# A decoder layer on one core: attention and w_out's first half put in an order written by hand

## Chip, core and metric

One core of one Trainium2 chip runs the whole layer in one launch. The metric is the device time of one execution in microseconds, the median over several runs.

## What is computed

One decoder layer on x of 512 positions by 1024 channels, in float32, cut to what matters here:

```python
h = rms_norm(x, g_pre_mix)
q, k, v, xr, gr = split(h @ w_in, ...)              # five parts of 512 columns
logits = q @ k.T * 64**-0.5 + bias[t5_bucket(q_pos - k_pos)]   # 8 heads of 64, causal
attn = softmax(logits) @ v
lru  = rg_lru(causal_dwconv(xr)) * gelu(gr)         # recurrent group
x = x + rms_norm(concat([attn, lru]) @ w_out, g_post_mix)
h = rms_norm(x, g_pre_ffn)
x = x + rms_norm((gelu(c_g) * c_u) @ w_down, g_post_ffn)       # c_u, c_g = conv3(h @ w_up)
```

With 512 positions and blocks of 256, of which up to three past ones are picked, the block-sparse attention of the reference is ordinary causal attention.

## The kernel before

**Products.** Every float32 operand of a product is held as two parts, an upper one (a rounded copy, made by ScalarE) and a lower one (the difference, made by VectorE): `split`, and for weights `split_w`. A product is then three matmuls, upper by upper, upper by lower and lower by upper (`mm3`, lines 79 to 81). Weights come by DMA into one of two `raw` buffers and are split into one of four `wh` and four `wl` slots.

**Stages.** Input norm and transposition into hT; the recurrent group's projection, convolution and gates; v; gr; then attention (up to line 702), the output product w_out in two halves of 512 columns (`wide`, for n = 0 and 1) with the post-norm, and the feed-forward part (w_up, w_down). Everything up to line 578 stands in an order written by hand for TensorE, ScalarE, VectorE and SP (`manual_schedule`, closed by `written.close()`). From there on a planner that estimates costs decides the order in which each engine gets its instructions.

**Attention.** Heads go in four pairs. `head_pair(pr)` loads the bias rows `tb` and the pair's q and k weights, splits the weights, makes 2 x 8 projection products (24 matmuls for q, 24 for k), and casts: q into its upper half (ScalarE) and lower half (VectorE), k into two copies of the upper half (ScalarE) and the lower half `klz` (VectorE), for each head s = 0, 1. A tile is 128 query positions of one head: 32 tiles (pr, s, i), and tile i sees 128 (i + 1) keys. `softmax` (lines 629 to 648) makes two score matmuls, adds the bias and takes the row maximum (one VectorE instruction, L640), negates and scales the maximum (L643), exponentiates with row sums (ScalarE, L644), takes the reciprocal (L646) and multiplies (L647, here the quotient). `transposed` turns the tile by TensorE (i + 1 transposes into `ptp`) and splits it into `pTh` and `pTl`. After the four tiles of a head `attend` makes eight value matmuls into `pav`, copies one half (ScalarE) and adds the other (VectorE) into `pair`, and splits `pair` into mixT.

The loop over the 32 tiles makes scores LAG = 3 tiles ahead of their transposes, and after each of them takes FILL = 3 projection products of the next pair. The products of w_out's first half (`py`, 4 row blocks x 8 k x 3 matmuls, banks "mm", "mm", "mm", "av") follow in program order; the planner may move them forward.

**PSUM.** Eight banks: three "mm" (projections, w_out), two "sc" (scores), two "tr" (transposes), one "av" (values).

**After attention.** `wide` for n = 1 splits the second half's weights, runs t by t, and `mixed` makes each row block's post-norm, the norm before the feed-forward part and its transposes into h2T. In between `load_first_up` loads and splits the first weights of w_up (`fw00` to `fw11`).

Of the kernel before, what the change touches and what calls it, by code (L numbers as in the profile page):

```python
# [39 lines left out]
ISCALE = DH ** -0.5  # L40
FE = S + P
EW = 3 * P
FILL = 3
LAG = 3
assert MAX_DISTANCE <= P

# [6 lines left out]
def hybrid_layer(  # L53
# [515 lines left out]
    for t in range(NT):  # L569
        pg = bank("pgr", "mm")  # L570
        for k in range(KD):
            mm3(pg, at(w_gr[t], slice(None), k), at(hT, slice(None), k), k == 0, k == KD - 1)
        if t >= 2:
            first_w.append(split_w(first_qk[:, :, t - 2], KD, P))
# [17 lines left out]
    heads = {}  # L592
# [5 lines left out]
    def head_pair(pr):  # L598

        tb = ap_.tile([P, 2, S], F32, tag="tb", name="tb")  # L600
# [6 lines left out]
        if pr:  # L607
            raw = load_qk(pr)
        ws = [split_w(raw[:, :, i], KD, P) for i in range(2)] if pr else first_w
        yield  # L610

        proj = []
        for w in ws:
            pq = bank("pq", "mm")
            for k in range(KD):
                mm3(pq, at(w, slice(None), k), at(hT, slice(None), k), k == 0, k == KD - 1)
                yield
            proj.append(pq)
        qs, ks = (ap_.tile([P, 2, S], F32R, tag=f"s{i}", name=f"s{i}") for i in "qk")
        kl = klz  # L620
        for s in range(2):
            me, other = own[s], own[1 - s]
            nc.scalar.copy(qs[me, s], proj[0][me])
            nc.vector.tensor_sub(qs[other, s], proj[0][me], f32(qs[me, s]))
            nc.scalar.copy(ks[me, s], proj[1][me])
            nc.scalar.copy(ks[other, s], proj[1][me])
            nc.vector.tensor_sub(kl[me, s], proj[1][me], f32(ks[me, s]))
        heads[pr] = qs, ks, kl, tb

    def softmax(pr, s, i):  # L630

        qs, ks, kl, tb = heads[pr]
# [3 lines left out]
        nc.tensor.matmul(psc[:, :W], qs[:, s, qi], ks[:, s, :W], start=True, stop=False)
        nc.tensor.matmul(psc[:, :W], qs[:, s, qi], kl[:, s, :W], start=False, stop=True)
        st = ap_.tile([P, S], F32, tag="st", name="st", bufs=4)
        sm = ap_.tile([P, 12], F32, tag="sm", name="sm", bufs=4)
# [7 lines left out]
        nc.vector.tensor_scalar(st[:, :W], st[:, :W], sm[:, 3:4], None, op0=ALU.mult)  # L647
        return st

    def transposed(st, pT, i):  # L650
        ptr = bank("ptp", "tr")
        for j in range(i + 1):
            nc.tensor.transpose(ptr[:, j * P:(j + 1) * P], st[:, j * P:(j + 1) * P], ident)  # L653
        split(by_keys(pT[0], i), by_keys(pT[1], i),
              ptr[:, :P * (i + 1)].rearrange("p (j q) -> p j q", q=P))

    def attend(pr, s, pT, pair):
        me, other = own[s], own[1 - s]
        pav = bank("pav", "av")
        for j in range(NT):  # L660
            vs = vhl[:, j, pr, 2 * s:2 * s + 2].rearrange("p a d -> p (a d)")
            for i in range(2):
                nc.tensor.matmul(  # L663
                    pav[:, j * P:], vs, pT[i][:, j * S:j * (S - P) + S],
                    start=j == 0 and i == 0, stop=j == NT - 1 and i == 1)
        nc.scalar.copy(pair[me], pav[other])
        nc.vector.tensor_add(pair[me], pav[me], pair[me])
        if s == 1:
            split(mixT[0][:, pr], mixT[1][:, pr], pair)

    tiles = [(pr, s, i) for pr in range(NPAIR) for s in range(2) for i in range(NT)]
    for _ in head_pair(0):
        pass
    ahead, sts, last = iter(()), [], None
    for n in range(-LAG, len(tiles)):
        if 0 <= n + LAG < len(tiles):
            pr, s, i = tiles[n + LAG]
            if s == 0 and i == 0:  # L680
                for _ in ahead:
                    pass
                if pr + 1 < NPAIR:
                    ahead = head_pair(pr + 1)
                    next(ahead)
            sts.append(softmax(pr, s, i))
        for _ in itertools.islice(ahead, FILL):
            pass
        if n < 0:
            continue  # L690
        pr, s, i = tiles[n]
        if i == 0:
            if last:
                attend(*last)
            if s == 0:
                pair = ap_.tile([P, S], F32, tag="pair", name="pair", bufs=1)
            pT = [ap_.tile([P, 3 * (S - P) + S], F32R, tag=f"pT{j}", name=f"pT{j}", bufs=1)
                  for j in "hl"]
            last = pr, s, pT, pair
        transposed(sts.pop(0), pT, i)  # L700
# [198 lines left out]
```

## Time and profile before

| | |
|---|---|
| median of 3 runs | 585.64 us (584.77 to 586.01) |
| profiled execution | 584.45 us |
| its span, first to last instruction | 582.3 us |
| TensorE matmul busy | 571.0 us (98%), 2734 matmuls |
| VectorE / ScalarE / GpSimd busy | 360.1 / 279.3 / 15.9 us |
| granted TensorE clock, mean | 0.996 |

The profile shows one execution. Matmul rows are longer than the distance of their starts, since matmuls are pipelined, so a busy share near 100% can hold waits; distances of starts show them. Releasers are inferred from semaphore events.

### The profile page before, as it was taken

What the parts mean: (1) busy time and instruction counts of PE and PEld (TensorE: products, weight loads), DVE (VectorE), ACT (ScalarE), POOL (GpSimd) and SP (SyncE); (2) the same over time, 40 slices, a digit from 0 to 9 for tenths busy, and PEclk for the clock granted to TensorE, in tenths of its full rate; (3) what the DMA queues carried; (4) which work ended last, traced back from release to release, by engine and by line L of the source; (5) the groups of instructions that cost most, each with busy time, mean ns of one, the idle gap of its engine ahead of it and who ended that gap; (6) DMA issues with size and microseconds to landing.
All of it is one profiled execution on the core that took longest, in us unless ns stands there. A gap on an engine that the chain in (4) does not pass through costs nothing.

```text
span 582.3 us, 7051 instructions
## 1 busy us (share of the span) xinstructions
PE 571.0 (98%) x2734; PEld 472.9 (81%) x2734; DVE 360.1 (62%) x649; ACT 279.3 (48%) x457; POOL 15.9 (3%) x37
## 2 busy tenths in 40 slices
PE   8999999999999999999999999999999999999995
PEld 4988887887788789888888888888888888888884
DVE  5797777889896895656656656656656521241225
ACT  6568846868776663543443444444444321132121
POOL 2150000000000000000000000000000000000000
PEclk9999999999999999999999999999999999999998
DMA  9533627333202614013412412412413222332103
GB/s 275 152 110 122 205 72 200 94 106 108 74 1 72 217 41 142 1 49 96 145 55 90 144 60 86 146 64 81 144 66 136 88 72 90 100 136 73 37 0 144
DMA packets 53450, 59.62 MB, mean 102 GB/s; under 512 B 2481, under 2 KB 42625, under 8 KB 53418
## 3 DMA queue, kind: packets, MB, share of 16 engines
q1 hardware_dynamic: 53319, 59.11, 31.9%
q8 instruction: 21, 0.34, 0.2%
q14 instruction: 12, 0.09, 0.1%
q10 hardware_dynamic: 98, 0.07, 0.0%
HBM read 57.06 MB, written 3.69 MB: 104 GB/s over the span
## 4 chain that ended last, share of the span: by engine, by line
PE 90%; DVE 4%; ACT 3%; DMA 2%; issue 0%; DVEq 0%; SPq 0%; ACTq 0%
PE pup L80 14%; PE pup L81 14%; PE pup L79 14%; PE py L80 8%; PE py L79 8%; PE py L81 8%; PE px L309 3%; PE pq L79 2%; PE pq L80 2%; PE pq L81 2%; PE pav L663 2%; PE ptp L653 1%; PE pgr L81 1%; PE pgr L80 1%; PE pv L81 1%; PE pv L80 1%
## 5 line engine op out<-in xcount | busy, mean ns | idle before, releaser
L85 DVE TENSOR_TENSOR wl<-raw,wh 128x1024 fp32r<-128x1024 f32 x78 | 95.3, 1222 | 125.4 <-ACT wh L84 125.1
L84 ACT CAST wh<-raw 128x1024 fp32r<-128x1024 f32 x78 | 81.7, 1049 | 139.7 <-PE py L81 71.7
L80 PE MATMUL pup<-h2Tl,wh 128*128 128x512 f32 x320 | 124.5, 389 | 0.0
L81 PE MATMUL pup<-h2Th,wl 128*128 128x512 f32 x320 | 124.5, 389 | 0.0
L79 PE MATMUL pup<-h2Th,wh 128*128 128x512 f32 x320 | 124.3, 389 | 0.0
L80 PEld LDWEIGHTS pup<-h2Tl,wh 128*128 128x128 f32 x320 | 60.1, 188 | 12.5
L79 PEld LDWEIGHTS pup<-h2Th,wh 128*128 128x128 f32 x320 | 60.0, 188 | 12.5
L81 PEld LDWEIGHTS pup<-h2Th,wl 128*128 128x128 f32 x320 | 60.1, 188 | 12.3
L79 PE MATMUL py<-wh,acth 128*128 128x512 f32 x176 | 68.5, 389 | 0.0
L80 PE MATMUL py<-wl,acth 128*128 128x512 f32 x176 | 68.5, 389 | 0.0
L81 PE MATMUL py<-wh,actl 128*128 128x512 f32 x176 | 68.5, 389 | 0.0
L79 PEld LDWEIGHTS py<-wh,acth 128*128 128x128 f32 x176 | 33.0, 188 | 6.9
L81 PEld LDWEIGHTS py<-wh,actl 128*128 128x128 f32 x176 | 33.0, 188 | 6.9
L80 PEld LDWEIGHTS py<-wl,acth 128*128 128x128 f32 x176 | 33.0, 188 | 6.7
L821 DVE SCALAR_TENSOR_TENSOR yu<-pup,par,yu 128x511 f32<-128x511 f32 (+1 forms) x44 | 32.9, 749 | 4.3 <-ACT yu L819 3.5
L828 ACT ACTIVATE yg<-yg 128x512 f32<-128x512 f32 x22 | 13.9, 632 | 44.6 <-DVE yg L821 44.6
L821 DVE SCALAR_TENSOR_TENSOR yg<-pup,par,yg 128x511 f32<-128x511 f32 (+1 forms) x44 | 32.8, 746 | 2.0 <-ACT yg L819 1.2
L829 DVE TENSOR_TENSOR yu<-yu,yg 128x512 f32<-128x512 f32 x22 | 15.2, 693 | 18.0 <-ACT yg L828 18.0
L81 PE MATMUL py<-wh,mixTl 128*128 128x512 f32 x64 | 25.4, 397 | 0.0
L79 PE MATMUL pq<-hTh,wh 128*128 128x512 f32 x64 | 25.4, 397 | 0.0
L81 PE MATMUL pq<-hTh,wl 128*128 128x512 f32 x64 | 25.3, 395 | 0.0
L79 PE MATMUL py<-wh,mixTh 128*128 128x512 f32 x64 | 25.2, 394 | 0.0
(213 smaller groups left out, 938.2 us busy)
## 6 DMA issues: line engine op xcount, KB each, us to landing
raw<-in_w_up_dram SPq DMA_DIRECT2D x22, 1024.0 KB, 5.1
raw<-in_w_down_dram SPq DMA_DIRECT2D x10, 1024.0 KB, 5.3
raw<-in_w_in_dram SPq DMA_DIRECT2D x4, 1024.0 KB, 5.2
rawqk<-in_w_in_dram SPq DMA_DIRECT2D x8, 512.0 KB, 5.3
raw<-in_w_out_dram SPq DMA_DIRECT2D x4, 1024.0 KB, 5.6
raw<-in_w_in_dram SPq DMA_DIRECT2D x4, 512.0 KB, 9.1
out_dram<-yz SPq DMA_DIRECT2D x8, 256.0 KB, 2.0
xres<-in_x_dram SPq DMA_DIRECT2D x3, 512.0 KB, 5.8
```

Source lines behind the costliest of these rows:

```text
L79: nc.tensor.matmul(o, lh, rh, start=start, stop=False)
L80: nc.tensor.matmul(o, lh, rl, start=False, stop=False)
L81: nc.tensor.matmul(o, ll, rh, start=False, stop=stop)
L84: nc.scalar.copy(h, src)
L85: (sub or nc.vector).tensor_sub(l, src, f32(h))
L309: nc.tensor.matmul(p_x[t][:, cs], w_x[t][i == LH][:, k], hT[i == HL][:, k, cs], start=first and n == 0, stop=last and n == len(todo) - 1)
L653: nc.tensor.transpose(ptr[:, j * P:(j + 1) * P], st[:, j * P:(j + 1) * P], ident)
L663: nc.tensor.matmul(pav[:, j * P:], vs, pT[i][:, j * S:j * (S - P) + S], start=j == 0 and i == 0, stop=j == NT - 1 and i == 1)
L821: nc.vector.scalar_tensor_tensor(y[:, d:], pt[:, :S - d], w_conv_f(2 - d, blk), y[:, d:], op0=ALU.mult, op1=ALU.add)
L828: nc.scalar.activation(yg, yg, AF.Gelu_apprx_tanh)
L829: nc.vector.tensor_mul(yu, yu, yg)
```

## The change

GpSimd is given here as `nc.gpsimd`, VectorE as `nc.vector`. The written order, which ended after gr, now goes on through attention and through all of w_out's first half, and ends there. FILL is gone. `head_pair`, `softmax`, `transposed` and `attend` are cut into their steps; the loop names at every step n (-3 to 31) which steps are issued, for all engines in one text. One step stands for one tile n (transposes and halves) and for tile m = n + 3 (scores, maximum, exponential) and m - 1 (quotient).

- The negation L643 is gone: the maximum instruction now scales by -1/8 and takes the minimum, and the exponential scales by -1.
- Weights of pairs 2 and 3 and the four weight units of w_out's first half have their lower parts made by GpSimd (`w_split(..., nc.gpsimd)`, `out_split`): eight instructions. Those of pairs 0 and 1 stay with VectorE.
- q and k of the next pair are cast at chosen steps (o = n mod 8): q at o = 0 and 4, k at o = 3 and 6; their scores come at o = 5 and, for the second head, o = 1.
- The halves of a head's first tile come one step later (`late`), behind the value products of the head before.
- w_out's first half: loads at steps 5 and 13, splits at 15, 16, 19 and 24, products at steps 19 to 31 and after the loop; the fourth row block is in an "sc" bank.
- Pair 1's q and k weights are loaded right after pair 0's, two biases at the start.
- The second half's `wide` gets the banks "sc", "av", "mm", "mm"; the four drains of the first half (`weighted`) stand outside `wide`.

```diff
-    first_qk = load_qk(0)
+    raw_qk = {0: load_qk(0), 1: load_qk(1)}
...
-    written.close()
...
+    def w_split(pr, i, eng=None):
+        w_qk[pr, i] = split_w(raw_qk[pr][:, :, i], KD, P, eng)
...
+    def maxima(m):
+        pr, s, i = tiles[m]
+        W = P * (i + 1)
...
         nc.vector.tensor_tensor_reduce(
-            out=st[:, :W], in0=psc[:, :W], in1=tb[:, s, S - W:S], scale=1.0, scalar=NEG,
-            op0=ALU.add, op1=ALU.max, accum_out=sm[:, 0:1])
-        nc.vector.tensor_scalar(sm[:, 1:2], sm[:, 0:1], -ISCALE, None, op0=ALU.mult)
-        nc.scalar.activation(st[:, :W], st[:, :W], AF.Exp, scale=ISCALE, bias=sm[:, 1:2],
-                             accum_out=sm[:, 2:3])
+            out=sts[m][:, :W], in0=psc[m][:, :W], in1=tbs[pr][:, s, S - W:S], scale=-ISCALE,
+            scalar=-NEG, op0=ALU.add, op1=ALU.min, accum_out=sms[m][:, 0:1])
+
+    def exponentials(m):
+
+        st, sm = sts[m][:, :P * (tiles[m][2] + 1)], sms[m]
+        nc.scalar.activation(st, st, AF.Exp, scale=-1.0, bias=sm[:, 0:1], accum_out=sm[:, 2:3])
...
+    def out_split(u):
+        w_out0[u] = split_w(raw_out[u // 4][:, u % 4:u % 4 + 2], 2, 512, nc.gpsimd)
+
+    def out_piece(t, k):
+        if t not in p_out:
+            p_out[t] = bank(f"py{t}", "sc" if t == 3 else "mm")
+        mm3(p_out[t], at(mixT, slice(None), k, slice(t * P, (t + 1) * P)),
+            at(w_out0[k // 2 * 2], slice(None), k % 2), k == 4, k == 3)
...
+    PIECES = (1, 3, 2, 2, 1, 3, 2, 2)
+    OUT = {19: ((0, 4), (0, 5)), 20: ((0, 6),), 21: ((0, 7), (1, 4), (1, 5)),
+           22: ((1, 6), (1, 7)), 23: ((2, 4), (2, 5)), 24: ((2, 6),), 25: ((2, 7), (0, 0)),
+           26: ((0, 1), (1, 0)), 27: ((1, 1), (2, 0)), 28: ((2, 1),), 29: ((0, 2), (1, 2)),
+           30: ((2, 2), (3, 4)), 31: ((3, 5), (3, 6))}
+    bias(0)
+    bias(1)
+    raw_qk[2] = load_qk(2)
+    pieces(0, KD)
+    w_split(1, 0)
+    cast_q(0, 0)
+    cast_q(0, 1)
+    w_split(1, 1)
+    raw_qk[3] = load_qk(3)
+    pieces(0, KD)
+    cast_k(0, 0)
+    pieces(1, 3)
+    late = None
     for n in range(-LAG, len(tiles)):
...
+        pr, o, m = n // 8, n % 8, n + LAG
+        if n >= 0:
+            turned(n)
+        if m < len(tiles):
+            scores(m)
+        if n >= 0:
+            if late is not None:
+                turned_halves(late)
+                late = None
+            if n > 0 and n % NT == 0:
+                late = n
+            else:
+                turned_halves(n)
+        nxt = pr + 2 if o >= 3 else pr + 1
+        if nxt < NPAIR:
+            pieces(nxt, PIECES[o])
+        for t, k in OUT.get(n, ()):
+            out_piece(t, k)
+        if n > 0 and n % NT == 0:
+            values(*tiles[n - 1][:2])
+        if m < len(tiles):
+            maxima(m)
+        if 0 <= m - 1 < len(tiles):
+            quotients(m - 1)
+        if o == 0:
+            if pr + 1 < NPAIR:
+                cast_q(pr + 1, 0)
+            if pr + 2 < NPAIR:
+                w_split(pr + 2, 0, nc.gpsimd)
+        elif o == 1 and pr > 0:
+            drain(pr - 1, 1)
+        elif o == 2 and pr > 0:
+            mix(pr - 1)
+        elif o == 3 and 0 <= pr < NPAIR - 1:
+            cast_k(pr + 1, 0)
+        elif o == 4:
+            if pr + 1 < NPAIR:
+                cast_q(pr + 1, 1)
+            if pr + 2 < NPAIR:
+                w_split(pr + 2, 1, nc.gpsimd)
+        elif o == 5 and pr >= 0:
+            drain(pr, 0)
+            if pr + 2 < NPAIR:
+                load_out(1 - pr)
+                bias(pr + 2)
+        elif o == 6 and pr + 1 < NPAIR:
+            cast_k(pr + 1, 1)
+        if m < len(tiles):
+            exponentials(m)
+        if n in (15, 16, 19, 24):
+            out_split({15: 4, 16: 6, 19: 0, 24: 2}[n])
+    values(NPAIR - 1, 1)
+    for k in (7, 0, 1, 2):
+        out_piece(3, k)
+    drain(NPAIR - 1, 1)
+    mix(NPAIR - 1)
+    for t in range(NT):
+        out_piece(t, 3)
+    written.close()
...
-    wide(w_out, mix_at, mix_ks, 0, 3, yg, gpost, ss, 1, lambda t, r: None)
-    wide(w_out, mix_at, mix_ks, 1, 3, yg, gpost, ss, 2, mixed, load_first_up)
+    for t in range(NT):
+        weighted(p_out[t], 0, yg[t], gpost, ss[t])
+    wide(w_out, mix_at, mix_ks, 1, 3, yg, gpost, ss, 2, mixed, load_first_up,
+         ("sc", "av", "mm", "mm"))
```

## Rows read from the trace of the kernel before

**Rows 1.** The page: the chain that ended last, shares by engine.

```profile
PE 90%; DVE 4%; ACT 3%; DMA 2%; issue 0%; DVEq 0%; SPq 0%; ACTq 0%
```

**Rows 2.** Stretches: length, then busy us and count of PE, PEld, DVE, ACT, POOL; PEclk.

```profile
87.98:187.57 99.59, 98.33 (x497) 79.93 (x496) 82.00 (x247) 71.51 (x156) 1.05 (x2) 1.00 0.30 90
119.07:138.65 19.58, 19.13 (x100) 15.59 (x100) 17.76 (x58) 15.03 (x36) 0.00 (x0) 1.00 0.25 78
138.65:158.25 19.60, 19.15 (x101) 15.60 (x101) 17.78 (x58) 15.03 (x36) 0.00 (x0) 1.00 0.28 80
187.57:210.70 23.13, 22.92 (x105) 18.58 (x103) 20.01 (x41) 16.24 (x28) 0.00 (x0) 1.00 0.49 160
```

**Rows 3.** Timeline of TensorE, pieces from five places: start, length, instruction.

```profile
97.73 0.39 PE L80 MATMUL pq<-hTl,wh 128*128 128x512 f32 x1
...
100.67 0.39 PE L81 MATMUL pq<-hTh,wl 128*128 128x512 f32 x1
...
118.66 0.27 PE L663 MATMUL pav<-pTl,vhl 128*128 128x128 f32 x1
119.07 0.33 PE L636 MATMUL psc<-sk,sq 128*128 128x128 f32 x1
...
123.94 0.60 PE L653 MATMUL ptp<-ident,st 128*128 128x128 f32 x4
...
124.85 0.40 PE L79 MATMUL pq<-hTh,wh 128*128 128x512 f32 x1
...
127.95 0.48 PE L663 MATMUL pav<-pTl,vhl 128*128 128x512 f32 x1
...
129.03 0.44 PE L81 MATMUL pq<-hTh,wl 128*128 128x512 f32 x1
```

**Rows 4.** Waits of TensorE's weight loads, 88 to 187.6: us in total, times, longest.

```profile
PEld pav L663 <- ACT pTh L84: 1.5, 5, 0.5
PEld ptp L653 <- DVE pTl L85: 1.5, 3, 0.6
```

**Rows 5.** Groups by line and shape, 109 to 178, VectorE, then ScalarE.

```profile
L85 DVE TENSOR_TENSOR wl<-raw,wh 128x1024 fp32r<-128x1024 f32 x4 | 4.9, 1216 | 0.0
L640 DVE CUSTOM_DVE_ANT_0 st<-psc,tb 128x512 f32<-128x512 f32 x7 | 4.8, 684 | 0.0
L646 DVE RECIPROCAL sm<-sm 128x1 f32<-128x1 f32 x29 | 4.7, 161 | 1.8 <-ACT st L644 1.6
L643 DVE TENSOR_SCALAR sm<-sm 128x1 f32<-128x1 f32 x29 | 4.2, 145 | 0.1
L647 DVE TENSOR_SCALAR st<-st,sm 128x512 f32<-128x512 f32 x8 | 3.9, 484 | 0.1
L647 DVE TENSOR_SCALAR st<-st,sm 128x128 f32<-128x128 f32 x7 | 2.0, 282 | 0.1
...
L644 ACT ACTIVATE st<-st,sm 128x512 f32<-128x512 f32 x8 | 5.8, 719 | 3.4 <-DVE sm L643 3.4
L84 ACT CAST wh<-raw 128x1024 fp32r<-128x1024 f32 x4 | 4.2, 1047 | 0.0
```

**Rows 6.** Timeline of GpSimd, then of VectorE, 9 to 20.

```profile
10.55 2.38 POOL L300 TENSOR_TENSOR wl<-raw,wh 128x1024 fp32r<-128x1024 f32 x1 [8.27 <-ACT wh L297]
17.35 2.39 POOL L300 TENSOR_TENSOR wl<-raw,wh 128x1024 fp32r<-128x1024 f32 x1 [4.41 <-ACT wh L297]
...
9.14 0.22 DVE L139 SCALAR_TENSOR_TENSOR rpre<-rpre 128x1 f32<-128x1 f32 x1
...
10.91 0.68 DVE L291 TENSOR_TENSOR hTl<-ptr,hTh 128x512 fp32r<-128x512 f32 x1
...
17.49 2.26 DVE L139 SCALAR_TENSOR_TENSOR rpre<-rpre 128x1 f32<-128x1 f32 x1
```

**Rows 7.** Waits of all engines, 187.7 to 232.

```profile
PEld pup L79 <- ACT h2Th L84: 0.9, 2, 0.5
ACT fw01h L84 <- DMA raw<-in_w_up_dram: 0.4, 1, 0.4
```

More of the change, by code (lines that the diff above doesn't have):

```diff
@@ L42 @@
 EW = 3 * P
-FILL = 3
 LAG = 3
@@ L573, in hybrid_layer @@
         if t >= 2:
-            first_w.append(split_w(first_qk[:, :, t - 2], KD, P))
+            first_w.append(split_w(raw_qk[0][:, :, t - 2], KD, P))
         nc.scalar.activation(gl[:, t], pg, AF.Gelu_apprx_tanh)
@@ L591, in hybrid_layer @@
     own = (slice(0, DH), slice(DH, P))
-    heads = {}
     klz = ap_.tile([P, 2, S], F32R, name="klz", bufs=1)
@@ L596, in hybrid_layer, with bias @@
         nc.gpsimd.memset(f32(klz[own[1 - s], s]), 0.0)
-    def head_pair(pr):
-        tb = ap_.tile([P, 2, S], F32, tag="tb", name="tb")
+    w_qk, p_qk, qkt, tbs, n_done = {(0, 0): first_w[0], (0, 1): first_w[1]}, {}, {}, {}, {}
+    def bias(pr):
+        tb = tbs[pr] = ap_.tile([P, 2, S], F32, tag="tb", name="tb")
         nc.sync.dma_start(tb[:, :, 0:S - 2 * P], bass.AP(
@@ L606, in head_pair @@
             ap=[[EW - 1, P], [P * EW, 2], [1, 2 * P]]))
[L607 to L632, printed above, removed]
+    def w_split(pr, i, eng=None):
+        w_qk[pr, i] = split_w(raw_qk[pr][:, :, i], KD, P, eng)
@@ new lines, in pieces, with qk_tiles @@
+    def pieces(pr, count):
+        for n in range(n_done.get(pr, 0), n_done.get(pr, 0) + count):
+            i, k = divmod(n, KD)
+            if k == 0:
+                p_qk[pr, i] = bank("pq", "mm")
+            mm3(p_qk[pr, i], at(w_qk[pr, i], slice(None), k), at(hT, slice(None), k),
+                k == 0, k == KD - 1)
+        n_done[pr] = n_done.get(pr, 0) + count
+    def qk_tiles(pr):
+        if pr not in qkt:
+            qkt[pr] = [ap_.tile([P, 2, S], F32R, tag=f"s{i}", name=f"s{i}") for i in "qk"]
+        return qkt[pr]
@@ new lines, in cast_q, with cast_k, scores @@
+    def cast_q(pr, s):
+        qs = qk_tiles(pr)[0]
+        me, other = own[s], own[1 - s]
+        nc.scalar.copy(qs[me, s], p_qk[pr, 0][me])
+        nc.vector.tensor_sub(qs[other, s], p_qk[pr, 0][me], f32(qs[me, s]))
+    def cast_k(pr, s):
+        ks = qk_tiles(pr)[1]
+        me, other = own[s], own[1 - s]
+        nc.scalar.copy(ks[me, s], p_qk[pr, 1][me])
+        nc.scalar.copy(ks[other, s], p_qk[pr, 1][me])
+        nc.vector.tensor_sub(klz[me, s], p_qk[pr, 1][me], f32(ks[me, s]))
+    def scores(m):
+        pr, s, i = tiles[m]
@@ L633, in softmax @@
         W = P * (i + 1)
-        psc = bank("psc", "sc")
+        qs, ks = qkt[pr]
+        psc[m] = bank("psc", "sc")
         qi = slice(i * P, (i + 1) * P)
[L636 to L639, printed above, removed]
-        nc.vector.tensor_tensor_reduce(
-            out=st[:, :W], in0=psc[:, :W], in1=tb[:, s, S - W:S], scale=1.0, scalar=NEG,
-            op0=ALU.add, op1=ALU.max, accum_out=sm[:, 0:1])
@@ L643, in softmax @@
-        nc.vector.tensor_scalar(sm[:, 1:2], sm[:, 0:1], -ISCALE, None, op0=ALU.mult)
-        nc.scalar.activation(st[:, :W], st[:, :W], AF.Exp, scale=ISCALE, bias=sm[:, 1:2],
-                             accum_out=sm[:, 2:3])
-        nc.vector.reciprocal(sm[:, 3:4], sm[:, 2:3])
[L647 to L653, printed above, removed]
+        nc.tensor.matmul(psc[m][:, :W], qs[:, s, qi], ks[:, s, :W], start=True, stop=False)
@@ new lines, in scores @@
+        nc.tensor.matmul(psc[m][:, :W], qs[:, s, qi], klz[:, s, :W], start=False, stop=True)
+    def maxima(m):
+        pr, s, i = tiles[m]
+        W = P * (i + 1)
+        sts[m] = ap_.tile([P, S], F32, tag="st", name="st", bufs=4)
+        sms[m] = ap_.tile([P, 12], F32, tag="sm", name="sm", bufs=4)
+        nc.vector.tensor_tensor_reduce(
+            out=sts[m][:, :W], in0=psc[m][:, :W], in1=tbs[pr][:, s, S - W:S], scale=-ISCALE,
+            scalar=-NEG, op0=ALU.add, op1=ALU.min, accum_out=sms[m][:, 0:1])
@@ new lines, in exponentials, with quotients, turned @@
+    def exponentials(m):
+        st, sm = sts[m][:, :P * (tiles[m][2] + 1)], sms[m]
+        nc.scalar.activation(st, st, AF.Exp, scale=-1.0, bias=sm[:, 0:1], accum_out=sm[:, 2:3])
+    def quotients(m):
+        st, sm = sts[m][:, :P * (tiles[m][2] + 1)], sms[m]
+        nc.vector.reciprocal(sm[:, 3:4], sm[:, 2:3])
+        nc.vector.tensor_scalar(st, st, sm[:, 3:4], None, op0=ALU.mult)
+    def turned(n):
+        ptp[n] = bank("ptp", "tr")
+        for j in range(tiles[n][2] + 1):
+            nc.tensor.transpose(
+                ptp[n][:, j * P:(j + 1) * P], sts[n][:, j * P:(j + 1) * P], ident)
@@ L654, in transposed, with turned_halves @@
+    def turned_halves(n):
+        pr, s, i = tiles[n]
+        if i == 0:
+            pTs[pr, s] = [ap_.tile([P, 3 * (S - P) + S], F32R, tag=f"pT{j}", name=f"pT{j}", bufs=1)
+                          for j in "hl"]
+        pT = pTs[pr, s]
         split(by_keys(pT[0], i), by_keys(pT[1], i),
[L655 to L659, printed above, removed]
+              ptp[n][:, :P * (i + 1)].rearrange("p (j q) -> p j q", q=P))
@@ L660, in attend, with values @@
+    def values(pr, s):
+        pav[pr, s] = bank("pav", "av")
         for j in range(NT):
@@ L663, in attend @@
                 nc.tensor.matmul(
-                    pav[:, j * P:], vs, pT[i][:, j * S:j * (S - P) + S],
+                    pav[pr, s][:, j * P:], vs, pTs[pr, s][i][:, j * S:j * (S - P) + S],
                     start=j == 0 and i == 0, stop=j == NT - 1 and i == 1)
[L666 to L669, printed above, removed]
-    tiles = [(pr, s, i) for pr in range(NPAIR) for s in range(2) for i in range(NT)]
@@ L674, in hybrid_layer @@
-    for _ in head_pair(0):
-        pass
-    ahead, sts, last = iter(()), [], None
-    for n in range(-LAG, len(tiles)):
[L678 to L700, printed above, removed]
@@ L701, in hybrid_layer, with drain, mix, load_out @@
-    attend(*last)
+    def drain(pr, s):
+        me, other = own[s], own[1 - s]
+        if s == 0:
+            pairs[pr] = ap_.tile([P, S], F32, tag="pair", name="pair", bufs=1)
+        pair = pairs[pr]
+        nc.scalar.copy(pair[me], pav[pr, s][other])
+        nc.vector.tensor_add(pair[me], pav[pr, s][me], pair[me])
+    def mix(pr):
+        split(mixT[0][:, pr], mixT[1][:, pr], pairs[pr])
+    raw_out, w_out0, p_out = {}, {}, {}
+    def load_out(c):
+        raw_out[c] = load_raw(w_out[c * 512:(c + 1) * 512, 0:512], 4, 512)
@@ new lines, in out_split @@
+    def out_split(u):
[5 more added lines that the diff above has]
+            at(w_out0[k // 2 * 2], slice(None), k % 2), k == 4, k == 3)
+    tiles = [(pr, s, i) for pr in range(NPAIR) for s in range(2) for i in range(NT)]
+    psc, sts, sms, ptp, pTs, pav, pairs = {}, {}, {}, {}, {}, {}, {}
@@ L736, in post_norm, with wide @@
                 nc.sync.dma_start(out[t * P:(t + 1) * P, hs], yg[:, hs])
-    def wide(src, x_at, ks, n, k_last, yg, g, ss, resident, done, held_split=None):
-        tags = ("mm", "mm", "mm", "av") if n == 0 else ("sc", "sc", "mm", "mm")
+    def wide(src, x_at, ks, n, k_last, yg, g, ss, resident, done, held_split=None, tags=None):
+        if not tags:
+            tags = ("mm", "mm", "mm", "av") if n == 0 else ("sc", "sc", "mm", "mm")
         py = [bank(f"py{t}", tags[t]) for t in range(NT)]
```

## The prediction, made before the change was run

> **What bounds the kernel now.** I read the chain that ended last first: TensorE holds 90% of it [rows 1], so only time in which TensorE waits can be won, or work taken from it. The change takes no TensorE instruction away. [...] The stretch that the change rewrites runs from the first q product at 87.98 to the last product of w_out's first half, where the second half's products begin at 187.57: 99.6 us. Busy shares say little of it, since the matmuls' rows overlap and hide waits; so I priced the work by starts. Fourteen 512-column products start within 97.73 to 100.67, 13 steps of 0.226. Four transposes and two 512-column scores take 123.94 to 124.85, 0.91, which is 4 x 0.113 + 2 x 0.227; the last seven of a head's eight value products take 127.95 to 129.03, 1.08, and the first 0.23 [rows 3]. Scores of 384, 256 and 128 columns I set at 0.18, 0.12 and 0.11 by their widths (an estimate from the 512 one; the two of 128 may not go below a transpose's 0.11).
>
> So four tiles of a head cost 10 x 0.113 = 1.13 in transposes, 2 x (0.227 + 0.18 + 0.12 + 0.11) = 1.27 in scores and about 1.27 in values (1.31 in the row, less what its neighbour was pushed): 3.67. A head pair with its 48 projection products costs 48 x 0.2266 + 2 x 3.67 = 18.2; it takes 19.6 in two of the stretches [rows 2]. The whole stretch holds 288 products of 512 columns (192 of q and k, 96 of w_out) and 8 heads: 65.3 + 29.4 = 94.7. The waits are 99.6 - 94.7 = **4.9 us: the most that a better order can win there.** One of them: a score that starts 0.41 after a 128-column value product instead of 0.1 [rows 3]; the waits name VectorE and ScalarE as those awaited [rows 4]. VectorE is busy 17.8 of 19.6 us of a pair [rows 2]: with nearly no reserve, each detour of its order reaches TensorE.
>
> **The change, part by part.**
> *Work taken from VectorE.* Per pair two lower weights (2 x 1.22) go to GpSimd and eight negations (8 x 0.145; `scale=-ISCALE` gives the negated maximum at once) disappear [rows 5]: 3.6 by durations, some 2.8 net of the 0.09 by which consecutive instructions overlap. 17.8 becomes 15.0 of 18.2. The reduction itself I cost as before (684 ns [rows 5]); it is the same instruction with other constants. Its cover is TensorE's 18.2, which leaves VectorE 3.2 us per pair.
>
> *The written order.* A step of TensorE is 18.2 / 8 = 2.3 us. Scores run three steps (6.8 us) ahead of their transposes; between them lie the maximum 0.68, exponential 0.72, reciprocal 0.16 and quotient 0.48 [rows 5], 2.1 with two steps to spare. k's halves are made two steps ahead of their scores, the halves of a head's first tile a step late so that ScalarE does not stand before the value products, whose operands TensorE's own step covers. Walking the list step by step with these durations I find TensorE waiting 0.3 us at w_out's third bank (step 23, freed by k's last half of step 22), and 0.2 before the last value products: 0.5 in all. After the last value products 12 products (2.7 us) cover copy, add and cast (three instructions on 512 columns, none over 0.72 [rows 5]), and the last 12 run behind them. Written queues also stand: on SP, pair 1's load goes out early, and w_out's loads stand before the biases of pairs 2 and 3, behind a buffer that GpSimd frees at step 5 or 13. The biases are needed eight steps (18 us) later. No cost. **Without any further wait: 94.7 + 0.5 = 95.2, 4.4 us less.**
>
> *GpSimd making eight lower weights.* One takes 2.39 us against VectorE's 1.22 [rows 5, 6], and waits only for its upper half; users come three or more steps later. The cost lies elsewhere. While GpSimd ran one (17.35 to 19.74 [rows 6]), a [128x1] VectorE instruction of 0.22 us took 2.26 and ended at 19.75, with GpSimd; a VectorE subtraction that reads PSUM and one SBUF tile beside another one (10.55 to 12.93) took its usual 0.68 [rows 6]. The blocked one reads two SBUF operands. The quotients (SBUF to SBUF, one tensor and a scalar) were never beside such GpSimd work before. Bounds: 0 as for the subtraction with PSUM, up to 2.4 each as for the blocked one. I take blocked: a quotient of 512 columns takes 484 ns, one of 128 282 [rows 5], so 384 more columns cost 202 ns, twice the speed of the PSUM reductions' 684 for 512, which means that it reads SBUF in a way no other instruction here does. [...]
>
> Where do the eight fall? At steps 0, 4, 8 and 12 ScalarE casts the weight before its exponential, and the next quotient needs that exponential and stands behind two lower halves: it meets only the last 0.5 us or so, and VectorE has 3.2 to spare per pair: no cost. The four of w_out are cast behind the exponential. Those of steps 15 and 16: a quotient waits some 1.4, TensorE 0.4. The one of step 24: 1.2, and TensorE nothing, as pair 3 has no casts left. The one of step 19 is a near tie. From the end of maximum 22 ScalarE has an exponential of 384 columns (about 0.6) and the cast (1.05 [rows 5]) before GpSimd starts: 1.7. VectorE has reciprocal, quotient, k's half, a 512 maximum, reciprocal: 0.16 + 0.35 + 0.69 + 0.68 + 0.16, less five overlaps of 0.09: 1.6 (the 0.35 lies between the quotients' rows, the 0.69 is taken as the maximum's). If GpSimd is first, quotient 22 stands 2.3 us, behind it q's half of pair 3, and behind that w_out's second bank, which TensorE wants in step 21: it waits 3.1. If the quotient is first, 0.8. I take GpSimd first, since each extra semaphore delays VectorE's five instructions more than ScalarE's two. **Sum: 94.7 + 0.5 + 0.4 + 3.1 = 98.7, 0.9 less than 99.6.**
>
> *What follows.* The second half's weights need the slots of the first half's, which now free only in the last 7 us (in the list, after the fourth row block's products), so four casts and lower halves (4 x 1.22) meet the four drains (4 x 0.75, an estimate: 512 columns and two one-column instructions each [rows 5]) at one time, some 2.5 us more VectorE work behind the half's end than before, and w_up's first load waits for a buffer about 3 us longer; the second load, for which ScalarE waits already [rows 7], hardly moves. VectorE is busy 20.0 of 23.1 us there [rows 2]: 3.1 idle can take it up. Bounds 0 and +2.4; I take +0.4, near the lower end.
>
> The profiled execution is 584.45 (span 582.3 and 2.15 around it), 1.2 under the median of 585.64. 584.45 - 0.9 + 0.4 = 583.95; on the median, **585.1 us**.
>
> **The rivals.**
> *Quotient first at step 19 (B).* Same mechanism, other winner of a tie of 0.1 us: 94.7 + 0.5 + 0.4 + 0.8 = 96.4, so 585.64 - 3.2 + 0.4 = 582.8. For it: the sums 1.7 and 1.6; against it: VectorE's longer list.
> *No block (C).* Quotients run beside GpSimd as the PSUM subtraction did: 585.64 - 4.4 + 0.4 = 581.6. Against it the 2.26 row and the quotient's speed.
> *The waits return behind w_out (D), slower.* Place: second half to the first w_up products. VectorE already ends that stretch late: TensorE's weight loads wait for h2T's casts [rows 7], and lower weights stand in front. If the drains go first, the third and fourth lower weights end about E + 5.5 (E: the first half's end) where TensorE wants the last at E + 4.1: 1.5 us; and a w_up half that lands late pushes the first norm by as much again: +3.0 in place of +0.4. 585.64 - 0.9 + 3.0 = 587.7. It decides from 2.1 us on. Against it the 3.1 idle.
>
> **How the numbers follow.** About 0.2% (1.2 us) is what a measurement of this kernel can tell from no change. Forecast (A) 0.44, its own range 583.9 to 586.4; B 0.30; C 0.10; D 0.16. Faster by over 0.2%: a fifth of A, nearly all of B and C: 0.09 + 0.25 + 0.09 = 0.43. Slower: most of D and a sixth of A: 0.15 + 0.07 = 0.22. Within: 0.35. The range reaches from C, which it holds only in its upper part, to just short of D's price: 581.4 to 587.3.
>
> **What would show it.** Right: two stretches of a pair near 18.2; eight GpSimd rows of 2.4; a quotient of over 2 us in step 20, and a product of w_out after it that starts about 3 us late, with VectorE's q half as the one awaited; first q product to second half about 98.7. B: the same quotient at 0.4 and a gap under 1. C: no quotient over 0.6 anywhere. D: weight loads of w_out's second half waiting for lower halves, and more than 2 us lost after it. Wrong altogether: pairs that still take 19.6, which would mean that the order, not VectorE's load, costs the waits.

## The result and the profile after

The changed kernel took **581.29 us** (median of 8 runs, 580.66 to 584.91), the kernel before beside it 584.99 (8 runs, 584.64 to 586.01): a ratio over all executions of 0.9948 [0.9924, 0.9972], 0.5% faster (that of the two medians is 0.9937). The median hides that the changed kernel has two times: two executions took 584.91 and 584.88, with a mean granted clock of 0.994 in both (here called the late kind), and six took 580.66 to 581.61, at 0.997 to 0.998 (the early kind). Nothing lies between. The profiled execution is one of the two (584.91, span 583.0), so the views below show the late kind. No execution of the early kind was profiled; experiment 2 shows a kernel made to be like it.

The chain that ended last, shares by engine, is still TensorE's [rows 1]:

```profile
PE 90%; DVE 3%; ACT 3%; DMA 2%; issue 1%; DVEq 0%; SPq 0%; ACTq 0%
```

The stretches (length, then busy us and count of PE, PEld, DVE, ACT, POOL; PEclk; DMA): first q product to w_out's second half; one pair of heads, from its first score to the next pair's; what follows w_out's first half [rows 2].

```profile
88.81:189.56 100.75, 97.49 (x498) 81.25 (x496) 77.60 (x201) 70.26 (x153) 20.14 (x10) 0.98 0.30 87
118.09:136.36 18.27, 18.27 (x103) 15.61 (x102) 15.94 (x48) 15.01 (x36) 4.80 (x2) 1.00 0.25 88
189.56:212.69 23.13, 22.77 (x105) 18.41 (x104) 21.05 (x48) 16.96 (x32) 0.00 (x0) 1.00 0.52 170
```

A pair with GpSimd's help has TensorE busy in all of its 18.27 us (a pair took 19.58 before), and VectorE is busy for 15.94 where it was for 17.8. (The pair behind it, with steps 15 and 16, takes 18.76, against 19.59.) Yet the whole stretch is 1.16 longer than before and its clock is 0.98. The waits of TensorE in it name the place:

```profile
PE py L78 <- DVE sq L628: 3.0, 1, 3.0
PE ptp L669 <- DVE st L664: 0.3, 1, 0.3
```

TensorE, start and length, around that wait:

```profile
155.90 0.40 PE L80 MATMUL py<-wh,mixTl 128*128 128x512 f32 x1
159.25 0.50 PE L78 MATMUL py<-wh,mixTh 128*128 128x512 f32 x1 [2.96 <-DVE sq L628]
159.59 0.39 PE L79 MATMUL py<-wl,mixTh 128*128 128x512 f32 x1
```

VectorE at the same time:

```profile
155.07 0.67 DVE L652 CUSTOM_DVE_ANT_0 st<-psc,tb 128x512 f32<-128x512 f32 x1
...
155.68 0.15 DVE L663 RECIPROCAL sm<-sm 128x1 f32<-128x1 f32 x1
155.86 2.61 DVE L664 TENSOR_SCALAR st<-st,sm 128x384 f32<-128x384 f32 x1
158.50 0.69 DVE L628 TENSOR_TENSOR sq<-pq,sq 64x512 fp32r<-64x512 f32 x1
```

And GpSimd, three of its seven rows:

```profile
145.09 4.75 POOL L84 TENSOR_TENSOR wl<-raw,wh 128x1024 fp32r<-128x1024 f32 x2 [6.15 <-ACT wh L83]
155.91 2.35 POOL L84 TENSOR_TENSOR wl<-raw,wh 128x1024 fp32r<-128x1024 f32 x1 [6.06 <-ACT wh L83]
169.85 2.39 POOL L84 TENSOR_TENSOR wl<-raw,wh 128x1024 fp32r<-128x1024 f32 x1 [11.60 <-ACT wh L83]
```

Read them together: quotient 22, 384 columns, lies beside GpSimd's lower weight and takes 2.61 us (0.42 without GpSimd); both end within 0.21 of each other; q's half stands behind the quotient, and the second bank of w_out behind q's half. Quotient and lower weight have recorded starts of 155.86 and 155.91: a tie of 0.05 us, in which the quotient even has the earlier start. That GpSimd was first is read from the quotient's 2.61. What comes next is in no row of before. The granted clock, in pieces of the same ten microseconds:

```profile
156.00:159.90 3.90, 0.94 (x5) 0.56 (x4) 3.84 (x5) 2.38 (x6) 2.25 (x1) 1.00 0.01 2
159.90:163.30 3.40, 3.40 (x12) 2.77 (x11) 1.77 (x6) 1.45 (x4) 0.00 (x0) 0.50 0.00 0
163.30:165.00 1.70, 1.70 (x11) 1.42 (x10) 1.49 (x6) 1.27 (x5) 0.00 (x0) 0.99 0.00 0
```

TensorE has work in all of 159.90 to 163.30 but at a granted clock of 0.50: 12 matmuls in 3.4 us, and 11 in the next 1.7.

VectorE's groups by shape, 109 to 178 [rows 5]:

```profile
L664 DVE TENSOR_SCALAR st<-st,sm 128x512 f32<-128x512 f32 x7 | 7.2, 1023 | 0.2
...
L652 DVE CUSTOM_DVE_ANT_0 st<-psc,tb 128x512 f32<-128x512 f32 x8 | 5.4, 681 | 0.1
...
L663 DVE RECIPROCAL sm<-sm 128x1 f32<-128x1 f32 x29 | 4.6, 157 | 0.0
L628 DVE TENSOR_TENSOR sq<-pq,sq 64x512 fp32r<-64x512 f32 x6 | 4.1, 688 | 0.8 <-ACT sq L627 0.6
...
L664 DVE TENSOR_SCALAR st<-st,sm 128x128 f32<-128x128 f32 x7 | 2.0, 287 | 0.2
```

Four rows of a form keep their times (684, 161, 282 before; q's half at 688); the negations and weights are gone; the 512-column quotients went from a mean of 484 to 1023, because six of the seven meet GpSimd: 1.07, 0.71, 0.86, 0.71, 1.78 and 1.54 us in the order of the stretch. Waits behind the stretch, 189.6 to 234 [rows 7]:

```profile
ACT fw01h L83 <- DMA raw<-in_w_up_dram: 1.2, 1, 1.2
...
PE ptr L159 <- DVE hn L153: 0.2, 1, 0.2
PEld pup L78 <- ACT h2Th L83: 0.2, 1, 0.2
...
PEld pup L79 <- DVE h2Tl L84: 0.2, 1, 0.2
```

From w_out's second half to the 97th w_up product it is 37.9 us, against 39.2 before: 1.3 won. VectorE's order there is another one. Before, w_up's second pair of lower weights stands between the two halves of the first residual sum:

```profile
196.25 0.75 DVE L733 SCALAR_TENSOR_TENSOR xres<-yg,rpost,xres 128x512 f32<-128x512 f32 x1
...
199.30 0.74 DVE L733 SCALAR_TENSOR_TENSOR xres<-yg,rpost,xres 128x512 f32<-128x512 f32 x1
```

In the changed kernel the two halves stand together, and the lower weights behind them:

```profile
198.25 1.41 DVE L830 SCALAR_TENSOR_TENSOR xres<-yg,rpost,xres 128x512 f32<-128x512 f32 x2
```

The part ahead of the stretch is 0.8 longer in this profile (88.81 for 87.98). That differs from one execution to the next: in the experiments' profiles with the same instructions ahead it is 87.67 to 88.71.

### The profile page after: what moved, and what is told of

Its sections match the earlier page's. It is cut to its first block, busy times and chain, and to the rows that moved or that the text cites. A ratio compares the mean times of both kernels' runs of the same rounds, so it can differ in the third digit from the quotient of the medians.

```text
span 583.0 us, 7046 instructions
## 1 busy us (share of the span) xinstructions
PE 570.2 (98%) x2734; PEld 474.7 (81%) x2734; DVE 356.7 (61%) x609; ACT 278.5 (48%) x457; POOL 35.0 (6%) x45
## 4 chain that ended last, share of the span: by engine, by line
PE 90%; DVE 3%; ACT 3%; DMA 2%; issue 1%; DVEq 0%; SPq 0%; ACTq 0%
PE pup L79 14%; PE pup L78 14%; PE pup L80 14%; PE py L80 8%; PE py L78 8%; PE py L79 8%; PE px L308 2%; PE pq L78 2%; PE pq L80 2%; PE pq L79 2%; PE ptr L159 2%; PE pav L686 1%; PE ptp L669 1%; PE pv L79 1%; PE pgr L79 1%; PE pv L78 1%
## 5 line engine op out<-in xcount | busy, mean ns | idle before, releaser
L84 DVE TENSOR_TENSOR wl<-raw,wh 128x1024 fp32r<-128x1024 f32 x74 | 90.5, 1223 | 124.5 <-ACT wh L83 124.3
L79 PEld LDWEIGHTS pup<-h2Tl,wh 128*128 128x128 f32 x320 | 60.1, 188 | 12.5
L80 PEld LDWEIGHTS pup<-h2Th,wl 128*128 128x128 f32 x320 | 60.1, 188 | 12.5
L79 PE MATMUL py<-wl,mixTh 128*128 128x512 f32 x64 | 25.6, 400 | 0.0
```

What stands on the lines that cost most here:

```text
L79: nc.tensor.matmul(o, lh, rl, start=False, stop=False)
L80: nc.tensor.matmul(o, ll, rh, start=False, stop=stop)
L84: (sub or nc.vector).tensor_sub(l, src, f32(h))
```

## The experiments

Each changes the changed kernel by the few lines shown, except the sixth, which changes the kernel before. The stretch is always from the first q product to w_out's second half.

**1 and 2: who wins the tie.** The theory is that the two times are the two ends of the tie at step 20: GpSimd first, or quotient 22 first. Experiment 1 delays the quotient:

```
-        nc.vector.reciprocal(sm[:, 3:4], sm[:, 2:3])
+        for _ in range(3 if m == 22 else 1):
+            nc.vector.reciprocal(sm[:, 3:4], sm[:, 2:3])
```

> The changed kernel with the reciprocal of tile 22 written three times (same value), so that VectorE reaches quotient 22 some 0.2 us later, at an instruction that is on nobody else's way. Theory (a tie of GpSimd's start and quotient 22 for a shared SBUF path decides each execution): GpSimd is always first, quotient 22 takes 2.3 us or more, TensorE idles about 3 us before w_out's second bank and then runs a stretch at half clock; all executions near 584.9, none near 581. Rival (the two times of the changed kernel come from somewhere else, such as DMA or start-up): both times still appear, median near 581.3.

Measured: 584.41 us (11 runs, 582.76 to 586.28), ratio 0.9993 [0.9984, 1.0002]. None is near 581, though they spread more widely than the theory had it. In the profile quotient 22 took 2.22 from 155.98, TensorE waited 3.1, 3.41 us at half clock followed; stretch 101.06.

Experiment 2 delays GpSimd: ScalarE casts 128 columns of the weight once more first.

```
+        if first:                       # 128 for unit 0 alone
+            nc.scalar.copy(h[:, 0, :first], src[:, 0, :first])
```

> The changed kernel with 128 columns of w_out's unit 0 cast once more before its whole cast on ScalarE (same value), so that GpSimd starts its lower weights some 0.2 us later. Theory: quotient 22 is always first and takes about 0.4 us, GpSimd waits 0.4 instead; TensorE's wait at w_out's second bank under 1 us, no half-clock stretch there; all executions near 581.0, 4 us under the kernel before. Rival: both times still appear, some near 584.9.

Measured: **581.09 us** (5 runs, 580.73 to 581.76), ratio 0.9938 [0.9926, 0.995]; stretch 97.88. VectorE, then GpSimd, at the place:

```profile
154.68 0.42 DVE L666 TENSOR_SCALAR st<-st,sm 128x384 f32<-128x384 f32 x1
155.61 0.69 DVE L630 TENSOR_TENSOR sq<-pq,sq 64x512 fp32r<-64x512 f32 x1 [0.52 <-ACT sq L629]
```

```profile
155.11 2.37 POOL L84 TENSOR_TENSOR wl<-raw,wh 128x1024 fp32r<-128x1024 f32 x1 [6.44 <-issue]
```

The quotient ends at 155.10 and GpSimd starts at 155.11, 0.13 behind the end of ScalarE's cast at 154.98, where it started 0.08 behind that in the changed kernel: now GpSimd is second. q's half beside GpSimd takes its usual 0.69. TensorE's waits from 140 to 175 and the granted clock (PEclk) of 155 to 165:

```profile
PE py L78 <- DVE sq L630: 1.3, 1, 1.3
PE ptp L671 <- DVE st L666: 0.3, 1, 0.3
PE py L78 <- DVE klz L637: 0.2, 1, 0.2
```

```profile
155.00:165.00 10.00, 8.55 (x45) 6.90 (x45) 7.59 (x24) 7.45 (x19) 2.37 (x1) 1.00 0.00 1
```

Both ends were made at will: none of 11 executions is early, none of 5 is late. (The mean clocks, 0.992 to 0.996 in experiment 1 and 0.996 to 0.999 in experiment 2, meet at 0.996 and do not tell the kinds apart in every execution.) So the tie decides between the two times. It is worth 584.41 - 581.09 = 3.3 us, though the waits at the bank differ by only 1.7 (3.14 and 1.42 by TensorE's starts; the 1.42 is over the 1 us hoped for); the stretches differ by 3.2. The other 1.5 would be the half clock, which experiment 8 takes up.

**3 and 7: is GpSimd needed at all?** Experiment 3 leaves all eight lower weights on VectorE, so that nothing can block a quotient; experiment 7 only the four of w_out.

```
-        w_out0[u] = split_w(raw_out[u // 4][:, u % 4:u % 4 + 2], 2, 512, nc.gpsimd)
+        w_out0[u] = split_w(raw_out[u // 4][:, u % 4:u % 4 + 2], 2, 512)
...
-                w_split(pr + 2, 0, nc.gpsimd)        (experiment 3 alone; also i = 1)
+                w_split(pr + 2, 0)
```

> The changed order with GpSimd taken out: all eight lower weights of pairs 2 and 3 and of w_out's first half are made by VectorE (1.22 us each, 1.13 net). Theory (order and the removed negations already win most; GpSimd's share is what opens the tie): VectorE near 17.3 of 18.2 us per pair, TensorE waits 1 to 2 us in all, no quotient over 0.6: 581 to 583, one time only. Rival (VectorE's relief is the gain): VectorE is again full, pairs at 19 or more, 584 to 586.

> The changed kernel with w_out's four lower weights made by VectorE; GpSimd keeps those of pairs 2 and 3. All on VectorE was 586.0. Theory (two lower weights at steps 15 and 16 and one at 19 are what overloads VectorE): TensorE still idles 2 us or more near step 18 and runs at half clock after it, 584 to 586. Rival (the pairs' lower weights had filled VectorE up and left it late for step 15): the wait falls under 1 us, 581 to 583.

Measured: experiment 3 took 586.04 us (10 runs), ratio 1.0025 [1.0015, 1.0034]: a miss, slower than before. TensorE's waits in it, 100 to 180, then the granted clock behind the longest:

```profile
PE ptp L669 <- DVE pTl L84: 3.3, 3, 2.7
PE py L78 <- DVE sq L628: 1.4, 1, 1.4
...
```

```profile
149.94:153.35 3.41, 3.00 (x10) 2.61 (x11) 3.28 (x13) 1.75 (x5) 0.00 (x0) 0.50 0.49 175
```

Experiment 7 took 584.83 (11 runs), ratio 1.0005 [0.9994, 1.0016]:

```profile
PE ptp L669 <- DVE pTl L84: 2.6, 2, 2.2
PE py L78 <- DVE sq L628: 2.0, 1, 2.0
...
```

Without any block VectorE is late by itself: in steps 15 to 19 it makes w_out's lower weights (1.22 each) beside k's and q's halves, and in experiment 7 TensorE waits 2.4 us at 147.5 and 2.1 at 157.7 by its starts. Its theory held but for the half clock: the granted clock stayed at 1.00 behind both waits. In a pair away from w_out VectorE alone still keeps up nearly: 18.74 in experiment 3 against 18.27 with GpSimd. So the written order without GpSimd is worth nothing here in all: its stretch is 102.91, 3.3 longer than before, and the part behind 37.7, 1.5 shorter. Most of the loss stays when w_out's four weights alone are VectorE's.

**6: GpSimd without the written order.** The planner's order of before, with GpSimd making the lower weights of pairs 2 and 3 and of w_out's first half, and the constants that spare the negation.

```
+        ws = [split_w(raw[:, :, i], KD, P, nc.gpsimd if pr > 1 else None)
+              for i in range(2)] if pr else first_w
...                                      (w_out's first half likewise; maxima as after)
```

> The kernel before with VectorE's relief alone: the planner's order stays, but GpSimd makes the lower weights of pairs 2 and 3 and of w_out's first half, and the negations are gone. Theory (the relief is what matters, the written order only places it): pairs come down from 19.6 towards 18.2, 581 to 583. Rival (a planner that knows nothing of blocked quotients loses it again): quotients of 2 us and more, waits of TensorE as before or longer, 584 to 587.

Measured: 586.84 us (6 runs), ratio 1.0036 [1.0024, 1.0048], as its rival had it. Three of the seven quotients of a head's second row block in this window (256 columns) are now blocked, at 1.9 us each (353 ns before), and TensorE waits 0.4 behind each of them:

```profile
L647 DVE TENSOR_SCALAR st<-st,sm 128x256 f32<-128x256 f32 x7 | 7.1, 1013 | 0.2
```

```profile
PE ptp L653 <- DVE pTl L85: 1.2, 3, 0.4
PE pav L663 <- ACT pTh L84: 0.2, 1, 0.2
```

A pair takes 20.2 there (19.6 before). VectorE is busy 0.9 us less per pair (16.87 for 17.78), blocked quotients included, and the kernel is slower. The waits that rows name are 1.4 us in its stretch, against 0.6 before, and the stretch is 2.3 longer (101.89); no row names the rest, so that the blocks cost all of it is not shown. Each part of the change loses or wins nothing alone; together they win.

**4 and 5: other places for the blocks.** Experiment 4 makes the casts of three w_out weights before the exponential of their step, and the third weight's a step later (20 for 19), so that GpSimd starts that one 0.75 us later, counted from the first score of pair 3; experiment 5 moves both q casts of pair 3 to steps 15 and 16 and the splits there to 13 and 15.

```
-        if n in (15, 16, 19, 24):                    (experiment 4)
+        if n in (16, 20, 24):   # stands before exponentials(m)
+            out_split({16: 6, 20: 0, 24: 2}[n])
...
+        if n in (15, 16):                            (experiment 5)
+            cast_q(3, n - 15)
...
+            out_split({13: 4, 15: 6, 19: 0, 24: 2}[n])
```

> The changed kernel with w_out's units 6, 0 and 2 split at steps 16, 20 and 24 ahead of the exponential, as the weights of pairs 2 and 3 are, so that the next quotient comes late enough by itself. Theory: no quotient over 1.1 us, TensorE waits under 1 us in the whole stretch, no half-clock stretch; 580 to 581, one time only, 0 to 0.8 under e2. [...]

> The changed kernel with pair 3's q halves cast at steps 15 and 16 instead of 16 and 20, and w_out's units 4 and 6 split at steps 13 and 15 instead of 15 and 16. Nothing then stands behind the blocked quotient of step 20 that TensorE wants soon. Theory: the 1.4 us before w_out's second bank that stay when the quotient is first, and the 0.45 at step 18, go; no half-clock stretch, whoever is first at step 20: 579.2 to 580.0, one time only, about 1.5 under the version in which the quotient is first (581.1). Rival (VectorE's total load, not the place of q's half, makes the wait): the wait returns at another place, 581 or more.

Measured: 581.46 us (5 runs), ratio 0.994 [0.9928, 0.9952], and 581.85 (5 runs), 0.9952 [0.994, 0.9965]. Both miss what was hoped, and neither has a second time. In experiment 4 quotient 22 takes 0.42 and quotient 26 is blocked in its place (2.62), where less stands behind it; quotient 19 is blocked as in the changed kernel (1.8). In experiment 5 quotient 18 is (2.4 at 145.7), and the wait is at the transposes behind it:

```profile
PE ptp L669 <- DVE pTl L84: 1.9, 1, 1.9
PE py L78 <- DVE klz L635: 0.3, 1, 0.3
```

Experiment 5 also shows how near the tie is. VectorE, then GpSimd, at step 20:

```profile
156.02 0.42 DVE L664 TENSOR_SCALAR st<-st,sm 128x384 f32<-128x384 f32 x1
```

```profile
156.07 2.63 POOL L84 TENSOR_TENSOR wl<-raw,wh 128x1024 fp32r<-128x1024 f32 x1 [8.19 <-PE pav L686]
```

The recorded starts are 0.05 apart, as in the changed kernel's profile, but here the quotient is first, and GpSimd's row is the longer one (2.63, otherwise 2.35 to 2.41).

**8: the half clock by itself.** Experiment 1 with the wait filled: 13 products of 512 columns with zero weights before the product that waits.

```
+            if n == 21 and (t, k) == (0, 7):
+                for _ in range(13):
+                    nc.tensor.matmul(p_out[0], klz[own[1], 0, 0:P], hT[0][own[1], 0], start=False, stop=False)
```

> The version in which GpSimd is first (584.4), with 13 matmuls of 512 columns by zero weights added to w_out's first row block at step 21, into the 3.1 us in which TensorE idles; they add nothing to the sums. Theory (the half-clock stretch after the idle time costs another 1.5 us): the granted clock stays at 1.00 and the time is 582.5 to 583.2. Rival (the idle time is all the cost): no gain, 584.2 to 584.8 or, if the fill runs over the wait, more.

Measured: 586.14 us (11 runs, 584.54 to 587.35), ratio 1.002 [1.001, 1.0031]. The clock of 155 to 165 in experiment 1, then in this:

```profile
155.00:165.00 10.00, 6.96 (x29) 5.19 (x27) 7.73 (x20) 6.04 (x15) 2.35 (x1) 0.83 0.00 1
```

```profile
155.00:165.00 10.00, 9.79 (x47) 7.32 (x46) 8.78 (x23) 6.09 (x16) 2.40 (x1) 1.00 0.00 1
```

The half clock is gone with the idle time, quotient 22 still takes 2.27, and the stretch falls from 101.06 to 99.79, by 1.27 of the 1.5 expected. That part held. The total did not: the part behind went from 37.84 to 41.21. The second w_up load was issued 1.77 us earlier (191.79 against 193.56), like everything there, but took 7.1 us to land instead of 5.2, TensorE waited 2.15 at 202.8 for the first norm behind it, and 3.41 us at half clock came after that wait:

```profile
205.93:209.34 3.41, 3.41 (x11) 2.75 (x10) 2.16 (x4) 2.81 (x7) 0.00 (x0) 0.50 0.24 77
```

Why the load took longer is not settled. Nor is this the whole of it: six executions took 586.14 to 587.35, the profiled one among them, and the other five 584.54 to 585.55, at mean clocks of 0.996 to 0.999. Not one came under experiment 1's median, so what the stretch wins shows in no total.

**9 and 10: take q's half off the quotient.** One move: pair 3's second q half is made in step 18. Experiment 10 has experiment 2's extra cast as well, and is the version meant to beat both kernels.

```
         elif o == 2 and pr > 0:
             mix(pr - 1)
+            if pr == 2:
+                cast_q(3, 1)
...
         elif o == 4:
-            if pr + 1 < NPAIR:
+            if pr + 1 < NPAIR - 1:
                 cast_q(pr + 1, 1)
```

> The changed kernel with one move: the second half of pair 3's q is converted in step 18 and not in step 20, so that it no longer stands behind quotient 22. Theory (the 3.0 us wait at w_out's second bank is that half's, and quotient 22 itself, even blocked for 2.6 us, has two steps to spare): the wait is under 0.5 us whoever wins the tie, no stretch at half clock follows, first q product to w_out's second half 97.0 to 97.9 us, 580.0 to 581.0 us in all executions, with none near 584.9. Rival 1 (the wait moves to another place, as when both halves were moved to steps 15 and 16, because VectorE or ScalarE has no free time in steps 18 and 19 either): a wait of 1.5 us or more elsewhere, 581.0 to 582.0. Rival 2 (a blocked quotient 22 holds the next step's halves as well): still two times, 3 us apart, the later one 583.5 to 584.9.

> The same move, and ScalarE casts 128 columns of w_out's third weight once more, so that quotient 22 wins the tie. This is the version meant to beat both kernels. Theory: the 1.42 us wait at w_out's second bank that was left when the quotient won falls under 0.3, stretch 96.6 to 97.3 us, 579.6 to 580.4 us, one time only. Rival 1 (the wait moves): stretch 97.8 or more, 581.0 us as without the move. Rival 2 (the earlier half delays the exponentials of steps 18 and 19): a wait for a quotient at the transposes of step 21 or 22 of 1 us or more, 581.5 us or later.

Measured: 581.76 us (5 runs, 580.89 to 582.81), ratio 0.9944 [0.9928, 0.9961], and 581.21 (5 runs, 580.88 to 582.38), 0.994 [0.9926, 0.9953]. In the profile of experiment 9 GpSimd came first again:

```profile
156.03 2.64 DVE L664 TENSOR_SCALAR st<-st,sm 128x384 f32<-128x384 f32 x1
158.59 0.61 DVE L84 TENSOR_TENSOR pTl<-ptp,pTh 128x128 fp32r<-128x128 f32 x2
```

TensorE's waits, 140 to 175, in experiment 9:

```profile
PE ptp L669 <- DVE pTl L84: 1.1, 1, 1.1
PE py L78 <- DVE klz L635: 0.7, 1, 0.7
```

and in experiment 10:

```profile
PE py L78 <- DVE klz L637: 1.2, 1, 1.2
PE ptp L671 <- DVE st L666: 0.3, 1, 0.3
```

In experiment 9, with q's half out of its way, the blocked quotient costs waits of 1.1 and 0.7 us, after which the clock stays whole, in place of 3.0 and a half clock. None of its five executions is near 584.9. But the wait moved, as its first rival had it (in two pieces, neither of the 1.5 us that it named), and the gain beyond 581 that the theories hoped for did not come: the same 1.2 to 1.3 us goes to k's half in experiment 10 as went to q's half in experiment 2. Five arrangements end within 581.1 to 581.9. No version here beats the early kind of the changed kernel; experiments 2 and 10 come within 0.2 us of its range in nine of ten executions (the tenth took 582.38), which the changed kernel does in six of eight.

## Why the prediction was right, and where only by luck

The forecast was made beside 585.64, the median of three executions; the kernel before is 584.99 over eight. Carried over by the ratio, 0.9948 of 585.64 is 582.6, within the range of 581.4 to 587.3; the bare 581.29 lies 0.1 below its lower end. The mechanism of the attention part held. The forecast's own case, A with 585.1, is not what most executions did: the median is that of the early kind, which is rival B (582.8, chance 0.30). Where 585.1 meets the late kind's 584.9, it does so by errors that cancel.

**Right.** TensorE's waits could be won: a pair takes 18.27 where 18.2 was forecast, with VectorE at 15.9 where 15.0 was (its blocked quotients are in the 15.9). Quotients are blocked by GpSimd, the open question between A, B and C: C is refuted by the 2.61, and D by the 1.3 won behind w_out. The places were right too: 0.46 lost behind steps 15 and 16 (forecast 0.4), nothing at steps 0 to 12 and 24 though those quotients took 0.7 to 1.5, and 3.0 at w_out's second bank (forecast 3.1). "A near tie" was literally so, and experiments 1 and 2 show both sides. That a quotient would be blocked was the author's estimate, from its 202 ns for 384 more columns and the 2.26 us of another instruction; the 2.61 shows the block, and no row shows what VectorE and GpSimd share.

**The choice in the tie.** The step that failed as put is "I take GpSimd first": in six of eight executions the quotient is, by their times; the tie's winner is read from a trace in the late kind alone. The reason given, that semaphores delay VectorE's longer list more, was the author's estimate without a number (one hand-over, from ScalarE's cast to GpSimd, took 0.08 us here), and it decided a difference of 0.1 us worked out from durations that are not that exact. What should have been forecast of a tie is two times, with the median on either side.

**Terms mis-sized.**
- Work, 94.7: with experiment 2's three waits over 0.25 us (1.42, 0.45 and 0.36) taken off, its 97.88 leaves 95.65. Either gaps too small to be listed make about 1 us, or the prices by starts were that much too low; no run separates the two.
- B's wait at the bank, 0.8: it is 1.42. In experiment 2 q's half waits 0.52 for ScalarE, which casts the weight and then q; the forecast had ScalarE free. But 0.28 of that is the cast that experiment 2 itself adds, so what the early kind of the changed kernel waits there is not measured.
- A's price: 3.1 of wait was right, but some 1.3 to 1.5 us of half clock came on top (experiment 8). The forecast has no term for the clock: in the stretches of before it stands at 1.00 [rows 2], and the longest wait listed for TensorE in the first of them is 0.3 us. So A's stretch is 100.75 where 98.7 was forecast, longer than before.
- The tail, +0.4 between 0 and +2.4: it is -1.3, outside its bounds. VectorE has 1.0 us more work there (21.05 for 20.01), not 2.5. w_up's first load is issued 0.5 us later against the half's end, not 3, and the second, which was hardly to move, is used 0.9 later (ScalarE waits 1.2 for it, not 0.4). But the planner put that work in another order: the two halves of the first residual sum stand together, so the first norm's sum of squares starts 11.1 us behind the half's end and not 12.5, and the gaps in front of h2T are gone. The profiles of all runs in the written order but experiment 8 have 37.6 to 37.9 there, without GpSimd too (experiment 3), and experiment 6 has 39.1: the 1.3 goes with the written order and its banks, not with GpSimd. Why the planner ordered so no experiment tested.

A's stretch 2.05 too short and the tail 1.7 too long: these two nearly make up for each other, and that is why 585.1 is so near to the 584.9 of the late kind. The 1.2 us that the forecast adds from the profiled execution to the median and the 0.8 that the part ahead of the stretch took longer do the rest; that these meet is luck too. For B, whose 582.8 stands against 581.1, the same tail is the greater part of the miss. In the profile of experiment 2 the span is 3.4 us shorter than before: 1.7 in the stretch, 1.3 behind it, 0.3 ahead of it. So of what the early kind wins, the part that was reasoned out is about half.

**What no step foresaw** is how little each half of the change is worth alone: the forecast priced the two together (4.4 us before the blocks) and neither by itself; experiment 3 shows the order lose 0.25% without GpSimd, since VectorE then has w_out's weights at steps where it has no time, and experiment 6 shows GpSimd lose 0.36% without the order.

## What to carry to other kernels

Before a lower weight goes to GpSimd, find the VectorE instructions that it holds up and what stands behind each in VectorE's order. In the changed kernel the quotients were held up (2.61 us instead of 0.42), a one-column reciprocal beside GpSimd was not (0.16 at 111.11), and the price was not the instruction's 2.4 us but the first thing behind it that TensorE wanted: a wait of 3.0 us behind quotient 22, none behind the quotient of 1.54 us at 170.98. When two instructions that hold each other up come due within some 0.1 us of each other, forecast two times, look for two in the runs, and then settle the order on purpose: one added cast of 0.28 us kept all five executions of experiment 2 from the late kind. And a wait of TensorE of 2 to 3 us can cost more than itself: look at the granted clock right after it (0.50 for 3.41 us behind the wait of experiment 1, of which filling that wait won 1.27 us of the stretch).

## What the runs showed of the hardware

- A SBUF-to-SBUF quotient and GpSimd's two-input subtraction held each other up, in both directions: quotient 22 took 2.61 us (changed kernel) and 2.22 (experiment 1) instead of 0.42 when GpSimd was first, and when the quotient was first, GpSimd started 0.01 us after its end (experiment 2) or took 2.63 instead of 2.40 (experiment 5). VectorE's subtraction with one operand in PSUM, q's half, took its 0.69 beside it (experiment 2).
- After TensorE had waited 3.1 us by its starts in the changed kernel and in experiment 1, 2.8 in experiment 3 and 2.15 in experiment 8, its clock stood at 0.50 for 3.41 us; after the 2.4 and 2.1 us of experiment 7 it stayed at 1.00. So in these runs the length of the wait alone does not decide it.
